# A hybrid attention and product-key layer on one core: three quarters of the modulation sums move from VectorE to column strips of TensorE

## The chip, the cores and the metric

The kernel runs on one core of one Trainium2 chip. The metric is the device time in microseconds (us) of one execution, as the median of several runs. Times inside the kernel come from one profiled execution; they are counted from its first instruction.

## What is computed

One decoder layer, float32, 256 tokens (T), width 2048 (D), weights read once from HBM. Cut to what matters here:

```python
c_act = jax.nn.silu(c)                              # one vector of 2048
mod = jnp.dot(c_act, w_ada) + b_ada                 # w_ada is 2048 x 12288, 96 MB
sh1, sc1, g1, sh2, sc2, g2 = split(mod, 6)          # 2048 each
h = layer_norm(x) * (1 + sc1) + sh1
mix = token_mix(h, ...)                             # w_in (32 MB), attention, w_o (16 MB)
x = layer_norm(alpha * x + g1 * mix, ln1_g, ln1_b)
h = layer_norm(x) * (1 + sc2) + sh2
ffn = peer(h, w_pq, ..., u_table, v_table)          # 16 MB, then two tables of 128 MB
out = layer_norm(alpha * x + g2 * ffn, ln2_g, ln2_b)
```

`token_mix` projects with `w_in` to the queries, keys and values of eight dilated heads ("a"), to the two latents of eight further heads ("b") and to a 64-wide rotary key (`kr`). `peer` scores every token against 128 x 128 keys, takes the top 16 of each head and mixes rows of `u_table` and `v_table`.

## The kernel before

**Products.** Two ways of multiplying float32 matrices stand side by side. In the split way, ScalarE (ACT) rounds a weight tile to `hi` (L98), VectorE (DVE) makes `lo = raw - hi` (L100), and TensorE (PE) makes three products (`mm3`, L137 to L139; for `u` two, L132 and L133). In the plain way PE multiplies the raw float32 tile (L330 for `w_in`, L147 and L154 for the latents), and ACT and DVE do nothing. A piece is 1 MB, 4 x 128 rows by 512 columns. `F32_PIECES = (4, 3, 2, 3)` says how many of the eight pieces of each of the four row groups (`kg`) of `w_in` go the plain way; `LAT_F32` names three latent products that do.

**Modulation.** `w_ada` comes as 96 tiles of 1 MB, one for each 128 of the 12288 outputs, with output on the partitions (`ada`, L203 to L209). DVE multiplies such a tile with `cb`, the silu of `c` spread over all partitions, and sums along the row: two SCALAR_TENSOR_TENSOR of 128x1024, whose sums go to `modc` and `modh`; `ada_bias` (L211 to L215) adds the halves and the bias. The tiles are spread over the program: 8 (shift and scale 1 of row group 0) before the first piece of `w_in`, 24 between its pieces for the groups 1 to 3, 48 (gate 1, shift and scale 2: `ada_rest`) pulled one at a time by `ada_pull` between pieces and heads, and the last of them in the `w_pq` stage, and 16 (gate 2) late, in the second half of the `u` stage. `modulate` (L294 to L307) makes `h` from the normalised x with them, and multiplies `h` with the 64 columns of `w_kr` into two PSUM banks.

**Order.** The stages are: x and `c` in; four row groups of `w_in` (`kg` 0 to 3); latents and attention; `w_o`; a layer norm; `w_pq`; then `u` and `v`, twice. The order of instructions on each engine is set by the framework's scheduler from the order of the text, the dependences and its own costs. All loads stand on one queue (SP), in order; a load waits until its buffer is free, and the loads behind it wait too. The `ada` tiles of `ada_rest` have two buffers. PSUM has eight banks: four `mm`, two `tr`, two `sm`.

The lines that the change and the prediction touch: `F32_PIECES`, `LAT_F32` (L41 and L50), `bank` (L70), `ada` (L203), `ada_rest` (L240), `modulate` (L294), `ada_in` and the calls behind it (L344 to L380), `latents` (L515), `scatter` (L892).

## Time and profile before

| | |
|---|---|
| time, median of 3 runs | 2075.01 us (2072.48 to 2075.48) |
| the profiled execution's own time | 2072.09 us |
| its span, first to last instruction | 2070.3 us |
| PE busy | 2002.6 us (97%) |
| DVE busy | 1434.0 us (69%) |
| ACT busy | 1027.9 us (50%) |
| HBM read | 473.4 MB, 239 GB/s over the span |
| mean granted clock of TensorE | 0.983 |

Busy shares are means over the whole span; the stages differ. Matmuls are pipelined, so that the records of neighbours overlap: the spacing of a run of matmuls is the price of one, and its mean duration is more than that. A float32 matmul of the plain way leaves two records (two passes, each with a weight load); one on split operands leaves one.

### The profile page before, as it was taken

To read this page: it belongs to the slowest core of one execution; us is meant where nothing else is said; L and a number is where in the kernel's file an instruction comes from. 1 tells how busy PE (TensorE), PEld (TensorE's weight loads), DVE (VectorE), ACT (ScalarE), POOL (GpSimd) and SP (SyncE) were. 2 spreads that over 40 slices of the span, in tenths; PEclk is the share of its full clock that TensorE was granted. 3 is DMA by queue.
4 is the path that set the end of the run, shared out by engine and by line. 5 is a ranking of instruction groups with operands and counts; after the bars stand their busy time and mean duration, and the time that the engine had idled before them with its cause. 6 is when DMAs were issued, how large, how long until landed. Compare 5 with 4: busy or idle time off the path is not lost.

```text
span 2070.3 us, 26806 instructions
## 1 busy us (share of the span) xinstructions
PE 2002.6 (97%) x10328; PEld 1672.8 (81%) x10329; DVE 1434.0 (69%) x2509; ACT 1027.9 (50%) x1478; POOL 0.2 (0%) x4
## 2 busy tenths in 40 slices
PE   6999998979999999999999999999999999999997
PEld 3567686769988888899888888888888888888886
DVE  7589978889799677677765454477766555445457
ACT  2323457445554877866444444454444454444441
POOL 0000000000000000000000000000000000000000
PEclk8999999989999999999999999999999999999999
DMA  9787887858445555666885555578876656555552
GB/s 364 314 328 311 328 323 262 345 234 318 184 157 190 194 212 193 224 204 214 291 280 190 198 188 198 188 266 306 300 286 244 224 205 235 192 202 184 203 203 102
DMA packets 100864, 496.13 MB, mean 240 GB/s; under 512 B 7792, under 2 KB 41728, under 8 KB 42880
## 3 DMA queue, kind: packets, MB, share of 16 engines
q1 hardware_dynamic: 100736, 494.41, 64.8%
q8 instruction: 81, 1.33, 0.2%
q14 instruction: 47, 0.39, 0.1%
HBM read 473.40 MB, written 20.98 MB: 239 GB/s over the span
## 4 chain that ended last, share of the span: by engine, by line
PE 93%; DVE 5%; ACT 1%; issue 0%; DMA 0%; SPq 0%; DVEq 0%; ACTq 0%
PE u_ps L132 23%; PE u_ps L133 12%; PE v_ps L138 11%; PE v_ps L137 11%; PE v_ps L139 11%; PE win_ps L330 3%; PE g_ps L914 3%; PE win_ps L138 2%; PE win_ps L139 2%; PE wpq_ps L138 2%; PE wpq_ps L139 2%; DVE ada L208 2%; PE wpq_ps L137 1%; PE win_ps L137 1%; PE wo_ps L139 1%; PE wo_ps L138 1%
## 5 line engine op out<-in xcount | busy, mean ns | idle before, releaser
L132 PE MATMUL u_ps<-act,hi_u 128*128 128x512 f32 x2048 | 727.8, 400 | 3.0 <-DVE W L779 3.0
L133 PE MATMUL u_ps<-act,lo_u 128*128 128x256 f32 x2048 | 574.0, 280 | 0.0
L100 DVE TENSOR_TENSOR lo_v<-raw_v,hi_v 128x1024 fp32r<-128x1024 f32 x244 | 298.2, 1224 | 264.4 <-ACT hi_v L98 264.3
L132 PEld LDWEIGHTS u_ps<-act,hi_u 128*128 128x128 f32 x2048 | 386.1, 189 | 95.2 <-DVE W L779 3.3
L100 DVE TENSOR_TENSOR lo_u<-raw_u,hi_u 128x1024 fp32r<-128x1024 f32 x256 | 312.1, 1222 | 179.8 <-ACT hi_u L98 178.8
L98 ACT CAST hi_v<-raw_v 128x1024 fp32r<-128x1024 f32 x244 | 257.2, 1054 | 327.8 <-PE v_ps L139 321.3
L133 PEld LDWEIGHTS u_ps<-act,lo_u 128*128 128x128 f32 x2048 | 387.6, 189 | 0.0
L137 PE MATMUL v_ps<-hi_v,whi 128*128 128x512 f32 x976 | 379.7, 389 | 0.0
L138 PE MATMUL v_ps<-lo_v,whi 128*128 128x512 f32 x976 | 379.7, 389 | 0.0
L139 PE MATMUL v_ps<-hi_v,wlo 128*128 128x512 f32 x976 | 379.7, 389 | 0.0
L98 ACT CAST hi_u<-raw_u 128x1024 fp32r<-128x1024 f32 x256 | 267.6, 1048 | 212.5 <-PE u_ps L132 193.4
L208 DVE SCALAR_TENSOR_TENSOR ada<-ada,cb 128x1024 f32<-128x1024 f32 x192 | 229.0, 1219 | 12.2 <-DMA ada<-in_w_ada_dram 12.0
L137 PEld LDWEIGHTS v_ps<-hi_v,whi 128*128 128x128 f32 x976 | 183.2, 188 | 38.3
L139 PEld LDWEIGHTS v_ps<-hi_v,wlo 128*128 128x128 f32 x976 | 183.2, 188 | 38.0
L138 PEld LDWEIGHTS v_ps<-lo_v,whi 128*128 128x128 f32 x976 | 183.2, 188 | 37.8
L330 PE MATMUL win_ps<-raw_win,hmod 128*128 128x512 f32 x192 | 87.2, 610 | 1.2 <-ACT hmod L301 1.2
L912 DVE TENSOR_SCALAR o<-iota,i2T,gT 128x128 f32<-128x128 f32 x256 | 72.9, 342 | 19.9 <-PE g_ps L914 19.8
L137 PE MATMUL wpq_ps<-act,hi_wpq 128*128 128x256 f32 x256 | 72.7, 286 | 1.9 <-ACT act L157 1.9
L138 PE MATMUL wpq_ps<-act,hi_wpq 128*128 128x256 f32 x256 | 73.1, 286 | 0.4 <-DVE act L158 0.4
L778 ACT COPY W<-u_ps 128x256 f32<-128x256 f32 x128 | 47.3, 369 | 52.3 <-PE u_ps L133 51.8
L139 PE MATMUL wpq_ps<-act,lo_wpq 128*128 128x256 f32 x256 | 72.8, 285 | 0.0
L330 PEld LDWEIGHTS win_ps<-raw_win,hmod 128*128 128x128 f32 x192 | 36.9, 196 | 43.8 <-issue 42.0
(319 smaller groups left out, 2316.1 us busy)
## 6 DMA issues: line engine op xcount, KB each, us to landing
raw_u<-in_u_dram SPq DMA_DIRECT2D x128, 1024.0 KB, 4.8
raw_v<-in_v_dram SPq DMA_DIRECT2D x122, 1024.0 KB, 4.8
ada<-in_w_ada_dram SPq DMA_DIRECT2D x96, 1024.0 KB, 5.9
raw_win<-in_w_in_dram SPq DMA_DIRECT2D x32, 1024.0 KB, 8.4
raw_wo<-in_w_o_dram SPq DMA_DIRECT2D x16, 1024.0 KB, 6.9
raw_wpq<-in_w_pq_dram SPq DMA_DIRECT2D x16, 1024.0 KB, 6.0
g_d<-stg SPq DMA_DIRECT2D x16, 1024.0 KB, 4.9
gl<-g_d SPq DMA_DIRECT2D x16, 1024.0 KB, 6.8
```

Of the source, the lines that this page charges most:

```text
L98: nc.scalar.copy(hi, raw[:, 2 * j:2 * j + 2, :])
L100: nc.vector.tensor_sub(lo, raw[:, 2 * j:2 * j + 2, :], hi.bitcast(F32))
L132: nc.tensor.matmul(pss[e], hi[:, i, es], act[:, k], start=first and j == 0 and i == 0, stop=False)
L133: nc.tensor.matmul(pss[e][:, 1], lo[:, i, es], act_hi[:, k, :], start=False, stop=last and j == 1 and i == 3)
L137: nc.tensor.matmul(o, sh, mh, start=start, stop=False)
L138: nc.tensor.matmul(o, sh, ml, start=False, stop=False)
L139: nc.tensor.matmul(o, sl, mh, start=False, stop=stop)
L208: nc.vector.scalar_tensor_tensor(w[:, z, :], w[:, z, :], 1.0, cb[:, z * 1024:(z + 1) * 1024], op0=ALU.mult, op1=ALU.mult, accum_out=(modc, ...
L330: nc.tensor.matmul(ps[th], act[:, i, ts], src[:, i, :], start=i == 0, stop=i == 3)
L778: nc.scalar.copy(ws[:, e], pss[e][:, 1])
L912: nc.vector.tensor_scalar(o2, iota, i2T[:, t:t + 1], gT[:, t:t + 1], op0=ALU.is_equal, op1=ALU.mult)
L914: nc.tensor.matmul(ps[:, q * P:(q + 1) * P], o1[:, q, :], o2, start=True, stop=True)
```

## The change

It touches four things.

1. `ada_group`: the 48 tiles of gate 1, shift 2 and scale 2 are laid out anew (`w_ada_r`: 128 rows x 4 row blocks x 512 columns, 1 MB a tile, 4 tiles for a group of 512 outputs). PE multiplies each row block of a tile (moving, 512 columns) with one column of `c1`, the silu of `c` (stationary, 1 column), into one row of a PSUM bank: row block g goes to partition 32 g, that is, to column strip g of the array. After 16 such matmuls ACT copies the bank to SBUF (`rows`), four small matmuls with `strips` (ones on the four partitions) add the strips and turn the row into columns, and DVE adds the bias.
2. `first_ada` does the same, in two halves, for the 8 tiles that come before the first piece of `w_in` (`w_ada0`, 256 columns, two strips for shift and two for scale). The 24 tiles of the row groups 1 to 3 and the 16 of gate 2 stay on DVE (`ON_PE = False`).
3. Seven pieces of `w_in` and the three latent products leave the plain way for the split one: `F32_PIECES` becomes (3, 1, 1, 0), `LAT_F32` becomes empty.
4. The bank `sm` is halved to one buffer and the other becomes `ad`, for the strips. So `kr` is now made transposed, in two strips of 64 columns in one bank (16 matmuls of 256 columns for 32 of 64), and turned back by two small matmuls; the heads' outputs (`o_`) have one bank for two; `scatter` uses `sm`, `tr`, `ad`, `tr` in turn.

```diff
-F32_PIECES = (4, 3, 2, 3)
+F32_PIECES = (3, 1, 1, 0)
+ON_PE = False
...
-LAT_F32 = ('uk0', 'uq1', 'uqr')
+LAT_F32 = ()
...
-        return psum.tile([P, 512], F32, tag=tag, name=name, bufs=4 if tag == "mm" else 2)
+        return psum.tile([P, 512], F32, tag=tag, name=name, bufs={"mm": 4, "tr": 2, "sm": 1, "ad": 1}[tag])
...
+    c1 = cols[:, V_C:V_C + KC]
...
+    def ada_group(ps, ws, tiles, strips, j0):
+
+        for q in range(4):
+            p, tag, bufs = tiles[q]
+            w = p.tile([P, 4, 512], F32, tag=tag, name=f"ada{j0}_{q}", bufs=bufs)
+            nc.sync.dma_start(w, ws[q])
+            for g in range(4):
+                nc.tensor.matmul(ps[32 * g:32 * g + 1, :], c1[:, 4 * q + g:4 * q + g + 1], w[:, g, :], start=q == 0,
+                                 stop=q == 3)
+            if q < 3:
+                yield
+        rows = stream.tile([P, 2, 512], F32, tag="lo", name=f"ada_rows{j0}", bufs=4)[:, 0, :]
+        nc.scalar.copy(rows, ps)
+        yield
+        for i in range(4):
+            nc.tensor.matmul(ps[:, 2 * i:2 * i + 2], rows[:, i * P:(i + 1) * P], strips[:, 2:4], start=True, stop=True)
+        one = 1.0 if (SC1 <= j0 < G1 or SC2 <= j0 < G2) else 0.0
+        nc.vector.scalar_tensor_tensor(modc[:, j0:j0 + 4], ps[:, 0:8:2], one, cols[:, j0:j0 + 4], op0=ALU.add,
+                                       op1=ALU.add)
+
+    def ada_rows(ps, w, which, half):
+
+
+        for i in range(8):
+            g = 32 * (2 * which + i % 2)
+            k = 8 * half + i
+            nc.tensor.matmul(ps[g:g + 1, :256], c1[:, k:k + 1], w[:, i, :], start=half == 0 and i < 2,
+                             stop=half == 1 and i >= 6)
...
         def ada_rest():
-            for j in range(G1, SH2):
-                ada(front, "ada", 2, j)
-                yield
...
+            order = [G1 + 4 * g for g in range(4)] + [j + 4 * g for g in range(4) for j in (SH2, SC2)]
+            for j0 in order:
+                yield from ada_group(ada_ps, a["w_ada_r"][j0 // 4], [(front, "ada", 2)] * 4, strips, j0)
...
                 for i in range(2 * half, 2 * half + 2):
-                    for th in range(2):
-                        nc.tensor.matmul(kr_ps[th][:, :64], h[:, i, th * P:(th + 1) * P], kw[:, i, :],
-                                         start=(kg == 0 and i == 0), stop=(kg == 3 and i == 3))
...
+                    g = 64 * (i % 2)
+                    nc.tensor.matmul(kr_ps[g:g + 64, :T], kw[:, i, :], h[:, i, :], start=(kg == 0 and i < 2),
+                                     stop=(kg == 3 and i >= 2))
...
-            for m in range(4):
-                ada_in(0, m)
+            first_ada(0)
             for n in range(2):
                 first[0, n] = load_piece(a["w_in"][0, n], f"win0_{n}")
-            for m in range(4, 8):
-                ada_in(0, m)
+            first_ada(1)
...
-                        ps = bank(("sm", "tr")[b % 2], f"g_ps{tb}_{b}")
+                        ps = bank(("sm", "tr", "ad", "tr")[b], f"g_ps{tb}_{b}")
```

What the diff does not show is where the new matmuls come to stand. The first place is PE in row group 3, between piece 7 and piece 0 of `w_in` (`win_ps3_n_th` is the bank of piece n and token half th). Before:

```order
L139 MATMUL win_ps3_7_1_1184<-hi_win3_7_1_1201,act_73 128x512
L137 MATMUL win_ps3_7_1_1184<-hi_win3_7_1_1201,act_73 128x512
L138 MATMUL win_ps3_7_1_1184<-lo_win3_7_1_1203,act_73 128x512
L139 MATMUL win_ps3_7_1_1184<-hi_win3_7_1_1201,act_73 128x512
L330 MATMUL win_ps3_0_0_1269<-raw_win3_0_1271,hmod3_1147 128x512 x2
L330 MATMUL win_ps3_0_1_1270<-raw_win3_0_1271,hmod3_1147 128x512 x2
```

And with the change:

```order
L139 MATMUL win_ps3_7_1_1327<-lo_win3_7_1_1346,act_73 128x512
L140 MATMUL win_ps3_7_1_1327<-hi_win3_7_1_1344,act_73 128x512
L233 MATMUL ada_ps_92<-ada32_0_1400,cols_67 1x512 x4
L233 MATMUL ada_ps_92<-ada32_1_1406,cols_67 1x512 x4
L596 MATMUL kr_ps_244<-both_1415,krT_1413 128x64 x2
L138 MATMUL win_ps3_0_0_1422<-hi_win3_0_0_1426,act_73 128x512
L138 MATMUL win_ps3_0_1_1423<-hi_win3_0_0_1426,act_73 128x512
L139 MATMUL win_ps3_0_0_1422<-lo_win3_0_0_1428,act_73 128x512
```

Two tiles of gate 1, four strip matmuls each, now stand in PE's row ahead of piece 0, which is now made from split operands.

The second place is PE in the `w_pq` stage, where the last tiles of `ada_rest` stand (`wpq_ps0` to `wpq_ps7` are the eight banks). Before there are only products of `w_pq`:

```order
L139 MATMUL wpq_ps1_3361<-act_73,lo_wpq0_1_0_3662 128x256
L137 MATMUL wpq_ps0_3360<-act_73,hi_wpq0_1_1_3664 128x256
L138 MATMUL wpq_ps0_3360<-act_73,hi_wpq0_1_1_3664 128x256
L139 MATMUL wpq_ps0_3360<-act_73,lo_wpq0_1_1_3666 128x256
L137 MATMUL wpq_ps0_3360<-act_73,hi_wpq0_1_1_3664 128x256
```

With the change:

```order
L233 MATMUL ada_ps_92<-ada76_1_4193,cols_67 1x512 x4
L233 MATMUL ada_ps_92<-ada76_2_4199,cols_67 1x512 x4
L138 MATMUL wpq_ps2_3813<-act_73,hi_wpq1_1_0_4227 128x256
L139 MATMUL wpq_ps2_3813<-act_73,hi_wpq1_1_0_4227 128x256
L138 MATMUL wpq_ps3_3814<-act_73,hi_wpq1_1_0_4227 128x256
L139 MATMUL wpq_ps3_3814<-act_73,hi_wpq1_1_0_4227 128x256
L233 MATMUL ada_ps_92<-ada76_3_4205,cols_67 1x512 x4
L241 MATMUL ada_ps_92<-strips_94,ada_rows76_4211 128x2 x4
L140 MATMUL wpq_ps2_3813<-act_73,lo_wpq1_1_0_4229 128x256
```

The load of tile `ada76_3` waits for the buffer that the matmuls on `ada76_1` give back, and only the four on `ada76_2` and four matmuls of 256 columns stand between; the four adding matmuls (L241) stand right behind the last strip matmul.

The third place is DVE in the same stage (`lo_wpqn_kg_j` is half j of a piece). Before:

```order
L100 TENSOR_TENSOR lo_wpq2_1_1_3812<-raw_wpq2_1_3804,hi_wpq2_1_1_3810 128x1024
L208 SCALAR_TENSOR_TENSOR ada78_3716,modc_71<-ada78_3716,cb_68 128x1024
L208 SCALAR_TENSOR_TENSOR ada78_3716,modh_72<-ada78_3716,cb_68 128x1024
L208 SCALAR_TENSOR_TENSOR ada63_3720,modc_71<-ada63_3720,cb_68 128x1024
L208 SCALAR_TENSOR_TENSOR ada63_3720,modh_72<-ada63_3720,cb_68 128x1024
L214 TENSOR_TENSOR modc_71<-modc_71,modh_72 128x4
L215 SCALAR_TENSOR_TENSOR modc_71<-modc_71,cols_67 128x4
```

With the change the two large instructions of a tile are gone; a group of four tiles leaves one small one:

```order
L101 TENSOR_TENSOR lo_wpq0_1_1_4143<-raw_wpq0_1_4135,hi_wpq0_1_1_4141 128x1024
L101 TENSOR_TENSOR lo_wpq1_1_0_4229<-raw_wpq1_1_4225,hi_wpq1_1_0_4227 128x1024
L243 SCALAR_TENSOR_TENSOR modc_71<-ada_ps_92,cols_67 128x4
L101 TENSOR_TENSOR lo_wpq1_1_1_4233<-raw_wpq1_1_4225,hi_wpq1_1_1_4231 128x1024
L101 TENSOR_TENSOR lo_wpq2_1_0_4294<-raw_wpq2_1_4290,hi_wpq2_1_0_4292 128x1024
```

The small instruction waits for PE's adding matmuls; the split of `w_pq` goes on around it.

## Rows read from the trace of the kernel before

**Rows 1.** The page's head: the span, and the busiest engine.

```profile
span 2070.3 us, 26806 instructions
PE 2002.6 (97%) x10328; PEld 1672.8 (81%) x10329; DVE 1434.0 (69%) x2509; ACT 1027.9 (50%) x1478; POOL 0.2 (0%) x4
```

**Rows 2.** Busy time by stage, 0 to 588 us; the first row names the columns.

```profile
core 0: us, PE busy (x) PEld busy (x) DVE busy (x) ACT busy (x) POOL busy (x), PEclk, DMA share, GB/s
0.00:28.00 28.00, 11.91 (x64) 9.98 (x64) 22.05 (x61) 10.41 (x18) 0.20 (x4) 0.82 0.85 340
28.00:90.00 62.00, 56.71 (x175) 34.02 (x176) 41.47 (x71) 20.95 (x33) 0.00 (x0) 0.92 0.85 340
90.00:142.00 52.00, 50.31 (x186) 33.34 (x185) 41.29 (x67) 13.52 (x17) 0.00 (x0) 1.00 0.86 351
142.00:196.00 54.00, 50.98 (x198) 36.26 (x197) 44.43 (x72) 17.14 (x20) 0.00 (x0) 0.97 0.84 342
196.00:251.00 55.00, 54.27 (x217) 37.16 (x217) 52.20 (x104) 23.55 (x42) 0.00 (x0) 1.00 0.71 271
251.00:342.00 91.00, 84.16 (x464) 65.55 (x462) 73.13 (x219) 55.45 (x133) 0.00 (x0) 0.98 0.81 313
342.00:450.00 108.00, 102.28 (x470) 83.17 (x469) 93.13 (x167) 53.36 (x77) 0.00 (x0) 0.97 0.77 302
450.00:475.00 25.00, 12.07 (x48) 8.30 (x48) 23.66 (x55) 15.69 (x26) 0.00 (x0) 0.65 0.46 177
475.00:588.00 113.00, 112.83 (x900) 110.98 (x900) 97.71 (x296) 56.17 (x70) 0.00 (x0) 0.99 0.62 234
```

**Rows 3.** Who waited, PE alone, 0 to 800 us: total, times, longest.

```profile
PE h_ps L712 <- ACT xc L709: 10.7, 2, 6.9
PE xnT_ps L291 <- issue: 9.4, 1, 9.4
PE win_ps L138 <- DVE lo_win L100: 5.6, 4, 2.9
...
PE pt_a L434 <- DVE mx_a L429: 4.9, 4, 3.6
```

**Rows 4.** The chain that ended last, runs of one kind: start, length, what.

```profile
90.39 1.73 PE kr_ps L306 x16
...
132.87 2.29 DVE ada L208 x4
...
258.00 1.73 PE uqr_ps L147 x4
...
270.86 1.73 PE uk_ps L154 x8
```

**Rows 5.** Busy time, `w_o` alone (400 to 425) and `w_pq` alone (500 to 525).

```profile
400.00:425.00 25.00, 25.00 (x112) 20.70 (x111) 22.69 (x30) 11.60 (x12) 0.00 (x0) 1.00 0.82 330
500.00:525.00 25.00, 25.00 (x208) 24.83 (x208) 19.15 (x29) 11.02 (x14) 0.00 (x0) 1.00 0.74 296
```

**Rows 6.** Timeline of PE, one score product: start, length, what.

```profile
285.32 0.70 PE L564 MATMUL s_b<-krT,qk 64*128 64x256 f32 x2
285.94 0.49 PE L561 MATMUL s_b<-qk 128*128 128x128 f32 x2
286.36 0.48 PE L562 MATMUL s_b<-krT,qk 64*128 64x128 f32 x2
286.78 0.70 PE L563 MATMUL s_b<-qk 128*128 128x256 f32 x2
```

**Rows 7.** Instructions on the tile `ada`, 0 to 600 us.

```profile
L208 DVE SCALAR_TENSOR_TENSOR ada<-ada,cb x160: 1161/1220/1226, 13.6 to 516.7; 128x1024 f32<-128x1024 f32 x160
...
DMA to landing us min/median/max: 4.7/6.7/15.2
```

**Rows 8.** Timeline of the start.

```profile
18.97 1.35 DVE L187 TENSOR_SCALAR xn<-xn,ln_mv,rs_r 128x2048 f32<-128x2048 f32 x1
...
27.51 1.09 ACT L301 ACTIVATE hmod<-xnT,modc 128x256 f32<-128x256 f32 x2
```

More of the change, by code (lines that the diff above doesn't have):

```diff
@@ L209, in ada, with silu_strips @@
                                            op1=ALU.mult, accum_out=(modc, modh)[z][:, j:j + 1])
+    c1 = cols[:, V_C:V_C + KC]
+    def silu_strips(pool):
+        ps = bank("ad", "ada_ps")
+        nc.vector.memset(ps, 0.0)
+        strips = pool.tile([P, 4], F32, name="strips")
+        nc.vector.memset(strips, 0.0)
+        for g in range(4):
+            nc.vector.memset(strips[32 * g:32 * g + 1, g // 2:g // 2 + 1], 1.0)
+            nc.vector.memset(strips[32 * g:32 * g + 1, 2:4], 1.0)
+        return ps, strips
+    def ada_group(ps, ws, tiles, strips, j0):
[3 more added lines that the diff above has]
+            nc.sync.dma_start(w, ws[q])
+            for g in range(4):
+                nc.tensor.matmul(ps[32 * g:32 * g + 1, :], c1[:, 4 * q + g:4 * q + g + 1], w[:, g, :], start=q == 0,
[16 more added lines that the diff above has]
+                             stop=half == 1 and i >= 6)
     def ada_bias(j0, n):
@@ L282, in tile_hybrid_peer_block @@
             nc.scalar.activation(cols[:, V_C:V_C + KC], cols[:, V_C:V_C + KC], AF.Silu)
+            ada_ps, strips = silu_strips(front)
             spread_cols(cb, cols[:, V_C:V_C + KC], "c")
@@ L297, in modulate @@
                 for j0 in (SH1, SC1):
-                    ada_bias(j0 + 4 * kg + 2 * half, 2)
+                    if kg > 0 and not ON_PE:
+                        ada_bias(j0 + 4 * kg + 2 * half, 2)
                 for i in range(2 * half, 2 * half + 2):
@@ L353, in ada_in, with first_ada @@
                 return ada((early_a, early_b)[m % 2], "raw", 1, j)
+            def first_ada(half):
+                ps = ada_ps
+                for part in range(2):
+                    ws = []
+                    for which in range(2):
+                        m = 4 * half + 2 * part + which
+                        where = (0, 2, 1, 0)[m // 2]
+                        pool, tag, bufs = ((front, "ada", 2), (mix, f"xt{m % 2}", 1),
+                                           ((early_a, early_b)[m % 2], "raw", 1))[where]
+                        w = pool.tile([P, 8, 256], F32, tag=tag, name=f"ada0_{m}", bufs=bufs)
+                        nc.sync.dma_start(w, a["w_ada0"][half, which, part])
+                        ws.append(w)
+                    for which in range(2):
+                        ada_rows(ps, ws[which], which, part)
+                rows = stream.tile([P, 2, 512], F32, tag="lo", name=f"first_rows{half}", bufs=4)[:, 0, :]
+                nc.scalar.copy(rows[:, :256], ps[:, :256])
+                for i in range(2):
+                    nc.tensor.matmul(ps[:, 256 + 2 * i:258 + 2 * i], rows[:, i * P:(i + 1) * P], strips[:, 0:2], start=True,
+                                     stop=True)
+                for which, (j0, one) in enumerate(((SH1, 0.0), (SC1, 1.0))):
+                    j = j0 + 2 * half
+                    nc.vector.scalar_tensor_tensor(modc[:, j:j + 2], ps[:, 256 + which:260:2], one, cols[:, j:j + 2],
+                                                   op0=ALU.add, op1=ALU.add)
             def group_start(kg):
@@ L375, in tile_hybrid_peer_block @@
                 m = 0
+                if ON_PE:
+                    slots = [(front, "ada", 2)] * 2 + [(mix, f"xt{m}", 1) for m in range(2)]
+                    work = [ada_group(ada_ps, a["w_ada_r"][j0 // 4 + kg + 1], slots, strips, j0 + 4 * kg + 4)
+                            for j0 in (SH1, SC1)]
+                    work = itertools.chain(*work)
                 for ns in IN_ORDER[kg]:
@@ L378, in tile_hybrid_peer_block @@
                     while m < ns[-1] + 1:
-                        ada_in(kg + 1, m)
+                        if ON_PE:
+                            next(work, None)
+                        else:
+                            ada_in(kg + 1, m)
                         m += 1
+                if ON_PE:
+                    for _ in work:
+                        pass
             early_pools.close()
@@ L529, in latents @@
                     nc.tensor.transpose(ps[:, th * P:(th + 1) * P], krd[:, th].rearrange("p j e -> p (j e)"), ident)
[L530 removed]
+                krT = krs
                 nc.scalar.copy(krT, ps[:, :T])
```

24 lines of the change are left out of this document (12 added, 12 removed).

## The prediction

> **What bounds the kernel now.** The page's head comes first: PE is busy for 2002.6 of 2070.3 us [rows 1], so only 68 us of the whole span are without PE work, and the reader should ask where these lie. The busy time by stage answers: the nine stages to 588 us add up to 535.5 us of PE, so 52.5 us of the 68 lie in this fifth of the span, 16 in the start and 13 in the layer norm at 450 [rows 2]. DVE is busy 489 us in the same stretch, but in no stage more than PE except the start and the layer norm. The list of waits then says what PE waited for. The two largest are chains of small steps (10.7 us for the normalised rows, 9.4 at the start); the waits for DVE's `lo` and for its share of the softmax come to 5.6 and 4.9 us [rows 3]. So DVE is nearly full and still holds PE up for only some 10 us; PE sets the pace, at a granted clock of 1.00 or nearly (2.4 GHz) in most stages; only the start and the layer norm, where PE had gaps, show 0.82 and 0.65, a mix of 1.2 and 2.4 GHz [rows 2]. What the change does to the time is therefore read from what it adds to PE and takes from it. From 588 us on nothing is added to PE; the turn of the banks in `scatter` gives each of its products a bank that was as long unused as before, so I cost that at nothing.
>
> **Prices.** In runs without waits the chain gives the plain way: 4 records of `uqr` in 1.73 us, 8 of `uk` in 1.73 [rows 4]. A matmul of 512 columns leaves two records, so it costs 0.86 us, one of 256 columns 0.43. Split operands: 112 matmuls in 25 us, 0.223 each for 512 columns, and 208 in 25 us, 0.120 for 256 [rows 5]. A matmul of 64 columns, plain, is 2 x 0.108 [rows 4]; there the weight load is the limit, so I use 0.22 for the small adding matmuls. An `ada` tile costs DVE 2.29 us [rows 4].
>
> **The change part by part.**
>
> Ten pieces off the plain way. A piece is 8 matmuls of 512 columns: 8 x 0.86 = 6.9 us plain, 24 x 0.223 = 5.4 split, 1.5 less. Seven pieces of `w_in` and `uqr` save 8 x 1.5 = 12.0. For `uk0` and `uq1`, 16 matmuls of 256 columns: 6.9 against 48 x 0.120 = 5.8, so 2.2 for both. **-14.2 us** of PE. DVE gets 20 `lo` for it, ACT 20 `hi`. In row groups 1 and 2 DVE goes from 41 and 44 us of 52 and 54 [rows 2] to about 46 and 47, still under PE; ACT has half of every stage free. Nothing for these.
>
> The key `kr`: 64 records at 0.108 = 6.9 us before; now 16 matmuls of 256 columns, 6.9 us one after the other or 3.5 if the two strips run together. **-3** (0 to -3.5).
>
> 48 tiles on strips: 192 matmuls of 512 columns with one stationary column. No row shows two strips at work, so the bounds are far apart: 192 x 0.86 = 165 us if they run one after the other, a quarter, **+41**, if four run together. I take 41: they use other columns of the array and other partitions of the bank, and the loads of weights already run beside matmuls (110.98 us busy beside 112.83 in `w_pq`, [rows 2]). What stands between the two is a rival below. The Trainium skill, "TensorE: Matmul & The Clock Gate" (Part 3), gives 2.38x for three column strips; at the same share of the ideal four would cost 52 us, 11 more, as an estimate; no run so far shows it.
>
> The adding matmuls: 48 at 0.22, **+10.5**.
>
> Changes of the array's shape. The score products switch between 64 rows and 128. The product of 256 columns over 64 rows starts at 285.32 and its successor at 285.94, 0.62 us for what costs 0.43 in the run of `uk`; the next ones take 0.42, where 0.22 would do [rows 4, 6]. So a switch costs 0.2 us. This is the rule that speaks against the change: the Trainium skill, "TensorEngine Tiling (Array Packing)" (Key Properties), says that changing the tiling mode drains the engine. The rows agree for strips of rows; by the rule this term would be 21 and the sum +52, without a drain nothing and the sum +31. The order of the changed kernel has 52 separate runs of strip matmuls among full ones, two switches each: 104 x 0.2 = 21 us. The stationary side is one column here and 128 there, which may make it cheaper. **+10** (0 to 21).
>
> Waits of PE for the tiles. DVE could fall behind a late tile; PE now stands still, and all its products behind. The load of a tile starts when the matmuls two tiles before are done, and lands after 6.7 us (4.7 to 15.2) [rows 7]. Counted in the order with the prices above, PE has over 6 us of work between the two in most cases, but 1 to 4 us in four, three of them in `w_pq` (one place is shown with the order): 2 to 5 us each. In three places the adding matmuls stand right behind the last strip, and wait for ACT's copy, some 1 us. **+10** (0 to 25).
>
> What DVE gives up: 56 tiles x 2.29 = 128 us. Of the 10.5 us that PE waited for DVE I take back most: **-8** (0 to -10.5). ACT's 14 extra copies and the single bank for the heads' outputs are hidden by the half of ACT that is free; without that cover the heads would wait some 0.5 us each, 8 us.
>
> The start. The normalising of x stood behind four tiles on DVE until 18.97, and the first `hmod` came at 27.51 [rows 8]. With the tiles on PE, which is idle there for 16 us [rows 2], only the loads remain: 2 MB of x and 4 MB of tiles at 340 GB/s are there by about 20. **-5** (0 to -8). The 64 small strip matmuls (64 x 0.43 / 4 = 7 us or more) lie in PE's idle time here; without that cover they are 7 us more.
>
> Sum: -14.2 -3 +41 +10.5 +10 +10 -8 -5 = **+41.3 us**. The profiled execution took 2072.1 us itself (span 2070.3), 2.9 under the median of 2075.0; with the change it would be 2113.4, and the median 2116.3. I say 2116. With all open terms at their low ends the sum is 41 + 10.5 - 14.2 - 3.5 - 10.5 - 8 = +15 (2090), at the high ends 41 + 10.5 - 14.2 + 21 + 25 = +83 (2158).
>
> **Rivals.**
>
> *The passes overlap only by halves.* Every plain matmul of the program is two records, x2 for one [rows 6], and the second pass of a strip needs the first out of the way. If PE starts them strictly in order, strip 1 starts with strip 0's second pass: a block of four takes five passes, 5 x 0.43 = 2.15 us for 0.86. 48 blocks cost 103 instead of 41: +62 on the sum, 2178. For it: the two records stand in program order; against it: nothing in the trace, it has no strips.
>
> *The strips do nothing.* The matmuls run one after the other, and the change does not do what it says: 165 for 41, 2240. Against it speaks that the shape is switched at all, since a switch is seen in the rows.
>
> *Faster: PE's waits close.* If DVE's load, not the chain of small steps, is what lies behind PE's gaps, the strips fill idle time instead of making the row longer. PE's net gain of work is +41 +10.5 -14.2 -3 = 34 us; there are 52.5 us of gaps to 588 [rows 2]. The point that decides is whether more than 34 of them close; if 47 do, the time is 13 less, 2062. For it: DVE at 80 to 95% in row groups and `w_o`, where a late `lo` stops PE. Against: 29 us of the gaps are the start and the layer norm, and the listed waits for DVE are 10.5 [rows 3].
>
> **How the numbers follow.** The measurement can tell about 0.2%, 4 us, from no change. Forecast 0.50, half overlap 0.21, no overlap 0.09, waits close 0.14, and 0.06 that terms cancel within 4 us: faster 0.14, same 0.06, slower 0.80. The range goes from 2060, which holds most of the faster case, over the forecast's own 2090 to 2158, to 2190, past the middle of half overlap; no overlap, and the far side of the two others, are left out, about 0.2.
>
> **What would show it.** In the profile after, the strip matmuls of one tile should start almost together and a block should take about 0.9 us, with a gap of some 0.2 on either side; 2.2 would be the first rival, 3.4 the second. PE's busy time to the `u` stage should grow by 35 to 60 us, most of it from row group 3 on, and that stage should begin near 630 instead of 588. DVE's should fall by some 100. In the list of waits, `ada_ps` waiting for its DMA should come to about 10 us, and PE's waits for `lo_win` be gone. If the `u` stage begins before 588, PE was not what bounded the front, and the reading of the stages was wrong.

## The result, and the profile after

The changed kernel takes 2148.3 us (median of 4 runs, 2145.8 to 2150.5) where the kernel before takes 2073.7 beside it on the same chip: a ratio of 1.036, with an interval of 1.0342 to 1.0378. The change costs 74.6 us. The forecast was 41.3, with the right sign and 2148 inside the range. What moved is 56 of the 96 tiles, 7 in 12, not the three quarters that the title names.

The page of the changed kernel, its head and the busy time of the engines, against [rows 1]:

```profile
span 2147.2 us, 28038 instructions
...
PE 2083.4 (97%) x11012; PEld 1701.9 (79%) x11013; DVE 1334.2 (62%) x2306; ACT 1055.9 (49%) x1513; POOL 0.2 (0%) x4
```

PE is busy for 80.8 us more than before, and DVE for 99.8 less. The span without PE work is 64 us; it was 68. So the change gave PE's row more work and closed hardly any of its gaps. The busy time by stage of the changed kernel, cut where the same instructions stand, shows in which stages this happened, against [rows 2]:

```profile
core 0: us, PE busy (x) PEld busy (x) DVE busy (x) ACT busy (x) POOL busy (x), PEclk, DMA share, GB/s
0.00:28.00 28.00, 19.75 (x132) 13.37 (x132) 14.29 (x53) 10.65 (x19) 0.20 (x4) 1.00 0.93 378
28.00:91.00 63.00, 59.45 (x243) 34.26 (x244) 33.95 (x53) 22.93 (x35) 0.00 (x0) 0.97 0.78 310
91.00:145.00 54.00, 49.30 (x197) 34.81 (x197) 46.54 (x73) 18.98 (x24) 0.00 (x0) 1.00 0.88 359
145.00:198.00 53.00, 49.04 (x196) 36.00 (x196) 46.71 (x74) 17.57 (x20) 0.00 (x0) 0.97 0.83 340
198.00:256.00 58.00, 56.54 (x284) 39.41 (x281) 37.87 (x69) 30.80 (x50) 0.00 (x0) 1.00 0.67 259
256.00:379.00 123.00, 118.27 (x738) 80.43 (x737) 48.48 (x178) 69.22 (x154) 0.00 (x0) 0.97 0.62 232
379.00:494.00 115.00, 112.99 (x562) 82.48 (x562) 65.63 (x106) 51.02 (x70) 0.00 (x0) 1.00 0.71 281
494.00:512.00 18.00, 9.81 (x51) 4.53 (x52) 16.78 (x45) 8.72 (x16) 0.00 (x0) 0.81 0.73 274
512.00:648.00 136.00, 125.27 (x921) 109.48 (x920) 65.92 (x191) 56.55 (x73) 0.00 (x0) 0.90 0.49 178
```

The start and the first three row groups are as long as before to 2 us: `kr` of group 3 begins at 197.6 (before 195.7). Then group 3 grows by 7 us, the attention by 23, `w_o` by 12. The layer norm stays. `w_pq` takes 136.5 us instead of 104.9, so it carries 32 of the 74. The `u` stage begins at 647.7 instead of 573.7, and from there to the end the two kernels differ by 3 us (1499.5 and 1496.6); in the kernels of this document, none of which differs there but by the banks of `scatter`, this part takes 1493 to 1501 us, so 3 us is no effect that can be told. The loss lies where the 48 tiles of `ada_rest` are pulled, as it should; but in `w_pq` it is largest, and there the granted clock is 0.90 where the same stage had 0.97 before. Over the whole stretch to the `u` stage the clock is not lower. Here it is in one row, first of the kernel before and then of the changed one:

```profile
0.00:573.70 573.70, 521.23 (x2626) 406.14 (x2628) 474.92 (x1038) 258.47 (x420) 0.20 (x4) 0.95 0.76 300
0.00:647.70 647.70, 600.13 (x3310) 434.50 (x3312) 375.87 (x835) 286.24 (x455) 0.20 (x4) 0.96 0.68 266
```

The kernel before has its half clock (1.2 GHz) mostly in the first 48 us and the layer norm, the changed one from the layer norm on. PE is busy at half clock for 36 us before and 42 after, so the clock costs 3 us more in all.

What PE waited for, 0 to 700 us, the largest entries of the changed kernel (total, times, longest), against [rows 3]:

```profile
PE win_ps L139 <- DVE lo_win L101: 9.8, 9, 3.4
PE h_ps L790 <- ACT xc L787: 8.7, 3, 6.3
PE ada_ps L233 <- DMA ada<-in_w_ada_r_dram: 6.3, 2, 3.2
...
PE ada_ps L241 <- ACT ada_rows L238: 3.9, 5, 1.6
```

The waits for `lo_win` were 5.6 us. They have grown, though DVE has 100 us less to do. New are the two entries on `ada_ps`: the strips wait for a tile, and the adding matmuls for ACT's copy. The instructions on that tile give the whole bill (name, records, their duration as minimum, median and maximum in ns, first and last start):

```profile
L233 PE MATMUL ada_ps<-ada,cols x384: 590/591/1061, 210.3 to 570.6; 128*1 128x512 f32 x192
...
L241 PE MATMUL ada_ps<-strips,ada_rows x96: 165/251/373, 228.6 to 573.8; 128*128 128x2 f32 x96
```

Taken from each record's start to the next one's, the strips hold PE for 72.2 us and the adding matmuls for 14.3. In 11.3 of the 72.2 PE stands idle behind a strip record, 8.2 of these in the layer norm, where its next product waits for ACT's `xc`; so 60.9 are work of the strips. The sections below take these apart.

### The profile page after: what moved, and what is told of

Its sections match the earlier page's. It is cut to its first block, busy times and chain, and to the rows that moved or that the text cites. A ratio compares the mean times of both kernels' runs of the same rounds, so it can differ in the third digit from the quotient of the medians.

```text
span 2147.2 us, 28038 instructions
## 1 busy us (share of the span) xinstructions
PE 2083.4 (97%) x11012; PEld 1701.9 (79%) x11013; DVE 1334.2 (62%) x2306; ACT 1055.9 (49%) x1513; POOL 0.2 (0%) x4
## 4 chain that ended last, share of the span: by engine, by line
PE 90%; DVE 5%; DMA 3%; ACT 1%; issue 1%; SPq 0%; DVEq 0%; ACTq 0%
PE u_ps L133 22%; PE u_ps L134 11%; PE v_ps L139 10%; PE v_ps L138 10%; PE v_ps L140 10%; PE g_ps L992 3%; PE ada_ps L233 2%; PE win_ps L139 2%; DMA gl<-g_d 2%; PE win_ps L140 2%; PE win_ps L138 2%; PE win_ps L368 2%; PE wpq_ps L140 2%; PE wpq_ps L138 1%; PE wpq_ps L139 1%; PE wo_ps L140 1%
## 5 line engine op out<-in xcount | busy, mean ns | idle before, releaser
L138 PEld LDWEIGHTS v_ps<-hi_v,whi 128*128 128x128 f32 x976 | 183.2, 188 | 37.9
L139 PE MATMUL win_ps<-lo_win,act 128*128 128x512 f32 x216 | 87.4, 405 | 10.2 <-DVE lo_win L101 9.8
L209 DVE SCALAR_TENSOR_TENSOR ada<-ada,cb 128x1024 f32<-128x1024 f32 x80 | 95.1, 1220 | 3.3 <-DMA ada<-in_w_ada_dram 3.2
L138 PE MATMUL win_ps<-hi_win,act 128*128 128x512 f32 x216 | 84.6, 406 | 2.5 <-ACT hi_win L99 2.5
L140 PE MATMUL win_ps<-hi_win,act 128*128 128x512 f32 x216 | 85.1, 394 | 0.0
L99 ACT CAST hi_win<-raw_win 128x1024 fp32r<-128x1024 f32 x54 | 54.8, 1050 | 53.2 <-DMA raw_win<-in_w_in_dram 36.7
L138 PE MATMUL wpq_ps<-act,hi_wpq 128*128 128x256 f32 x256 | 75.0, 295 | 0.0
L101 DVE TENSOR_TENSOR lo_win<-raw_win,hi_win 128x1024 fp32r<-128x1024 f32 x54 | 64.6, 1220 | 15.1 <-ACT hi_win L99 15.0
```

The source lines that it names most:

```text
L99: nc.scalar.copy(hi, raw[:, 2 * j:2 * j + 2, :])
L101: nc.vector.tensor_sub(lo, raw[:, 2 * j:2 * j + 2, :], hi.bitcast(F32))
L138: nc.tensor.matmul(o, sh, mh, start=start, stop=False)
L139: nc.tensor.matmul(o, sh, ml, start=False, stop=False)
L140: nc.tensor.matmul(o, sl, mh, start=False, stop=stop)
L209: nc.vector.scalar_tensor_tensor(w[:, z, :], w[:, z, :], 1.0, cb[:, z * 1024:(z + 1) * 1024], op0=ALU.mult, op1=ALU.mult, accum_out=(modc, ...
```

## Do the strips run together?

The forecast rested on it (41 us), and two rivals denied it (103 or 165). In the timeline of PE, one block in row group 3 of the changed kernel reads (start, length, what):

```profile
226.57 0.39 PE L140 MATMUL win_ps<-hi_win,act 128*128 128x512 f32 x1
226.89 1.04 PE L233 MATMUL ada_ps<-ada,cols 128*1 128x512 f32 x8
227.86 0.73 PE L138 MATMUL win_ps<-hi_win,act 128*128 128x512 f32 x2
```

Eight records, two for each of four strips, take 0.97 us from the first's start to the next product's, with what the switch costs. The starts of the eight show how: the first passes of the four strips begin 6 to 7 ns apart, then 408 ns later the four second passes begin, as close together. So the second pass of a strip doesn't hold back the first pass of the next one.

Not every block stays whole. Nine of the 48 are broken by other matmuls: one strip runs alone, and the other three follow later, as here in the attention:

```profile
259.77 1.02 PE L233 MATMUL ada_ps<-ada,cols 128*1 128x512 f32 x2 [0.32 <-DVE modc L243]
...
262.22 1.03 PE L233 MATMUL ada_ps<-ada,cols 128*1 128x512 f32 x6
```

The lone strip holds PE for 0.95 us and the three for 0.96, as long as a whole block. So the 48 blocks take 57 times two passes, 114 x 0.43 = 49 us and not the 41 of the forecast.

**One strip.** To see what the block costs without that, all sixteen matmuls of a group go into strip 0. The other three strips are then not written and keep what lay there; the work on PE is the same in number and size.

```diff
-                nc.tensor.matmul(ps[32 * g:32 * g + 1, :], c1[...], w[:, g, :], start=q == 0, stop=q == 3)
+                nc.tensor.matmul(ps[0:1, :], c1[...], w[:, g, :], start=q == 0 and g == 0, stop=q == 3 and g == 3)
```

> All 16 matmuls of a group of gate 1, shift 2 and scale 2 go to one column strip instead of four; the numbers of matmuls, copies and loads stay. If the four strips really ran together and this stands on the path (theory), 192 matmuls x 0.86 us come one after the other instead of four at a time: +124 us, about 2270 us, and a block of four takes 3.4 us instead of 0.9. If the loads or the waits of the tiles set the pace and not PE's time on them (rival), less than +40, below 2190.

It took 2235.7 us (one run; 2072.0 before beside it). The same place in PE's timeline:

```profile
236.08 0.39 PE L140 MATMUL win_ps<-hi_win,act 128*128 128x512 f32 x1
236.40 3.59 PE L233 MATMUL ada_ps<-ada,cols 128*1 128x512 f32 x8
239.92 0.50 PE L138 MATMUL win_ps<-hi_win,act 128*128 128x512 f32 x1
```

3.52 us instead of 0.97, records 428 to 429 ns apart. PE's time on L233 goes from 72.2 to 176.3 us, and the kernel takes some 87 us more than with four strips. That lies between the two expectations: PE's gaps ahead of the `u` stage close from 47.6 to 31.0 us, so part of the added time fills what was idle. Both rivals on the strips fall; four column strips gave four times the rate, 8 x 0.429 = 3.43 us of passes in about 0.86. The Trainium skill, "TensorE: Matmul & The Clock Gate" (Part 3), gives 2.38x for three column strips; for four float32 strips of one column these rows show 4.0, so its figure would have put 11 us too many on the sum for whole blocks.

**Half the columns.** The strip matmuls run over 256 of the 512 columns, so half of the sums are left out; loads, copies, adding matmuls and switches stay.

```diff
-                nc.tensor.matmul(ps[32 * g:32 * g + 1, :], c1[...], w[:, g, :], ...)
+                nc.tensor.matmul(ps[32 * g:32 * g + 1, :256], c1[...], w[:, g, :256], ...)
```

> The changed kernel with the strip matmuls of the 48 tiles over the first 256 of 512 columns alone: half of these sums are left out, so that the modulation is not the reference's. Loads, copies, adding matmuls and the number of switches stay; a block costs 0.43 us for 0.86. If PE's time on the strips is on the path (theory 1): 48 x 0.43 = 21 us faster than the changed kernel, 2128. If late tiles set the pace (theory 2): PE waits for what it saves, less than 8 us, above 2140.

2126.4 us, ratio 1.0259 [1.0241, 1.0278], against 1.036 for the change: 21 us of 2073 come back. The strip records, per instruction of this kernel:

```profile
L233 PE MATMUL ada_ps<-ada,cols x384: 377/377/631, 212.2 to 554.5; 128*1 128x256 f32 x192
```

Each is 0.214 us shorter, and 114 passes give 24 us of PE time. By the medians 21 come back, in the two profiled executions 17 up to the `u` stage (630.4 for 647.7), and not where the passes lie. Forty of the 48 blocks lie ahead of `w_pq`, some 20 us of the saving; that stage begins at 505.5 instead of 511.2, so only 5.7 of it arrive there. In `w_pq` lie eight blocks, some 4 us; the stage takes 124.9 instead of 136.5, 11.6 less. So ahead of `w_pq` part of the strips' time is covered (three blocks, 4.7 us of work, lie in the gaps of the layer norm), and in `w_pq` they cost more than their own length, which the section on the waits takes up.

**No adding.** The 48 adding matmuls go, and DVE takes every second of the first eight columns of ACT's copy in place of their sums, so the sums over the strips are left out.

```diff
-        for i in range(4):
-            nc.tensor.matmul(ps[:, 2 * i:2 * i + 2], rows[:, i * P:(i + 1) * P], strips[:, 2:4], start=True, stop=True)
...
-        nc.vector.scalar_tensor_tensor(modc[:, j0:j0 + 4], ps[:, 0:8:2], one, ...)
+        nc.vector.scalar_tensor_tensor(modc[:, j0:j0 + 4], rows[:, 0:8:2], one, ...)
```

> The changed kernel without the 48 adding matmuls: VectorE takes its columns from ScalarE's copy of the strips, so that the modulation of gate 1, shift 2 and scale 2 is not the reference's. Loads, strip matmuls and copies stay. In the profile after, the adding matmuls take 14.3 us of PE, and PE waits some 6 us for the copy ahead of them, partly at half clock. If their PE time and these waits are on the path (theory 1): 15 to 22 us faster than the changed kernel, 2126 to 2133. If they fill time that PE waits through anyway (theory 2): less than 6 us, above 2142.

2131.2 us, ratio 1.0285 [1.0267, 1.0303]: 15 us back (0.0075 of 2073). Again the sum is near what the records hold PE in the trace of the change, 14.3, and the places are others: `w_pq` begins 3.4 us earlier, though nine of the twelve groups lie ahead of it, and itself takes 120.8 us instead of 136.5. The busy time of this kernel over `w_pq` and its neighbours, to set beside the row 512 to 648 above:

```profile
512.00:635.00 123.00, 116.72 (x921) 105.52 (x921) 70.78 (x223) 56.09 (x70) 0.00 (x0) 0.97 0.53 193
```

The granted clock is 0.97 here and 0.90 in the change. Without the adding matmuls the tiles run otherwise against PE's row: PE waits 4.0 us for tiles in `w_pq` instead of 6.3, with one long wait instead of two. So this run measures the adding matmuls together with the waits that they help to bring about.

## Which part costs what

Five kernels take parts off the change, one, two or three of them. Each time is given with its ratio to the kernel before, run beside it.

**First eight tiles back on DVE.**

```diff
-                    if kg > 0 and not ON_PE:
+                    if not ON_PE:
...
-            first_ada(0)
+            for m in range(4):
+                ada_in(0, m)
...
-            first_ada(1)
+            for m in range(4, 8):
+                ada_in(0, m)
```

> The changed kernel with the first 8 tiles on VectorE again; the 48 tiles stay on strips, the ten pieces split, kr in strips. In the profile after, the second half of row group 0 began 4 us later than before, because the strip matmuls of the second four tiles stand behind w_in pieces 0 and 1 on PE. If that is what the first tiles cost (theory 1): about 4 us faster than the changed kernel, 2144. If PE gives the time back later (theory 2): no difference, 2146 to 2150.

2145.0, 1.0343 [1.0326, 1.0361]. On PE the first tiles cost some 3.5 us, within the two intervals; that they gain is not shown.

**The ten pieces plain again.**

```diff
-F32_PIECES = (3, 1, 1, 0)
+F32_PIECES = (4, 3, 2, 3)
...
-LAT_F32 = ()
+LAT_F32 = ('uk0', 'uq1', 'uqr')
```

> The changed kernel with the ten pieces in the plain float32 way again, as before. By PE's arithmetic of the prediction (theory 1) they cost PE 14 us more: 2162 us. If the split pieces only swap PE time for waits on DVE's lo and ACT's hi in the row groups (theory 2), no difference beyond 4 us, or faster: 2140 to 2152, with row groups 1 and 2 as long as now (53 us each).

2154.1, 1.0398 [1.0377, 1.0418]: splitting the ten pieces gains 8 us (0.0038 of 2073), with intervals that just overlap. It lies between the two expectations.

**The 48 tiles back on DVE,** the ten pieces split as in the change.

```diff
-            order = [G1 + 4 * g for g in range(4)] + [j + 4 * g for g in range(4) for j in (SH2, SC2)]
-            for j0 in order:
-                yield from ada_group(ada_ps, a["w_ada_r"][j0 // 4], [(front, "ada", 2)] * 4, strips, j0)
+            for j in range(G1, SH2):
+                ada(front, "ada", 2, j)
+                yield
+            ada_bias(G1, 16)
...
```

> The changed kernel with the 48 tiles of gate 1, shift 2 and scale 2 on VectorE again; the first 8 tiles stay on strips and the ten pieces stay split. If PE's time on the strips is the whole loss (theory 1) the 77 us go and the split pieces bring their 14: 2060 us. If split pieces and 48 tiles together are too much for DVE (theory 2: 20 lo more, 24 us, on an engine that was 80 to 95% busy from row group 0 to w_o), it lies above the kernel before: 2080 to 2100.

2084.3, 1.0064 [1.0044, 1.0084], as by the second theory. Against it the 48 tiles on strips, with the pieces split (1.036), cost 0.0296 of 2073, 61 us.

**The 48 tiles back and the pieces plain,** so that the first eight tiles, the key and the banks are left of the change.

```diff
-F32_PIECES = (3, 1, 1, 0)
+F32_PIECES = (4, 3, 2, 3)
...
-                yield from ada_group(ada_ps, a["w_ada_r"][j0 // 4], [(front, "ada", 2)] * 4, strips, j0)
+                ada(front, "ada", 2, j)
...
```

> The kernel before with only the first 8 tiles and kr on strips: the 48 tiles on VectorE and the ten pieces plain, as before. The prediction's term for the start (theory 1) says 5 us faster and kr 3: 2066 us. If the loads and not VectorE set the start (theory 2, the profile after shows the first w_in matmul at 28.2 as before), no difference beyond 4 us: 2070 to 2078.

2079.7, 1.0042 [1.003, 1.0054], above both expectations, with single executions from 2075.7 to 2084.2. Against this the 48 tiles on strips, with the pieces plain (1.0398), cost 0.0356 of 2073, **74 us**. And the ten pieces, split while DVE has the tiles (1.0064), cost 4.6 us, in intervals that overlap, instead of gaining 8: a gain shows only once DVE has lost the tiles.

**The key and the banks alone:** the same, and the first eight tiles back on DVE too.

```diff
-            first_ada(0)
+            for m in range(4):
+                ada_in(0, m)
...
```

> The kernel before with the bank change alone: kr transposed in two strips, one bank for the heads' outputs, scatter's banks in turn; all tiles on VectorE, the ten pieces plain. The kernel with the first 8 tiles on strips as well was 8 us slower than before. If those 8 us are the first tiles' (theory 1): no difference from before, 2069 to 2075. If the bank change costs (theory 2: one bank for the heads' outputs, a longer chain for krT): 2076 to 2080.

2076.1, 1.0011 [1.0001, 1.002], +2.3 us; inside what can be told from no change. In its trace `kr` itself does what was forecast: the eight records of a row group take 1.0 us where sixteen took 1.73 [rows 4], 2.9 us less for four groups. But turning the key back takes 0.6 us, and PE's waits ahead of `kr` grow from 3.5 to 5.0 us, so 0.8 of the 2.9 are left. What takes these and the 2.3, the single banks or something else, the runs don't tell. From here to the kernel with the first tiles too it is 6 us (0.0031 of 2073).

Taken in this order, each step from the kernel of the one ahead of it, the steps are +2 for banks and key, +6 for the first tiles, +74 for the 48 tiles and -8 for the pieces, which by construction is the whole 74.6. In another order the prices are others (61 instead of 74 for the tiles with the pieces split).

## Why the pieces gave so little

Four of them lie in row groups 0 to 2, three in group 3, three in the latent projections. Three kernels split these.

**Groups 0 to 2 plain again in the change.**

```diff
-F32_PIECES = (3, 1, 1, 0)
+F32_PIECES = (4, 3, 2, 0)
```

> The changed kernel with the four pieces of row groups 0 to 2 in the plain way again (4, 3, 2, 0); the three of group 3 and the three latent products stay split. The kernel with all ten back was 6 us slower, and its row group 3 began at 196.9 us against 197.6, so that the four seem to give nothing. If split pieces of these groups only swap PE time for waits on lo (theory 1): within 3 us of the changed kernel, 2145 to 2151. If PE's arithmetic holds there too (theory 2): 4 x 1.45 = 6 us slower, 2154.

2145.6, 1.0356 [1.0338, 1.0375]: no difference to 1.036. Four pieces, 6 us of PE work by the forecast, are worth nothing. The waits of PE in groups 1 and 2 show where it went, first of the changed kernel (91 to 198 us), then of the kernel before (90 to 196):

```profile
PE win_ps L139 <- DVE lo_win L101: 7.2, 4, 3.4
PE win_ps L138 <- ACT hi_win L99: 1.2, 2, 0.7
```

```profile
PE win_ps L138 <- DVE lo_win L100: 4.5, 2, 2.9
```

Groups 1 and 2 take 53 to 54 us in both kernels. In the change PE is busy 49 of these and DVE 46.5; the split pieces need a `hi` and a `lo` each, and they come later than PE could use them. Three pieces less are 4.5 us of PE work, and the waits grew by 7.2 + 1.2 - 4.5 = 3.9: the saved work became waiting. Beside the kernel with all ten plain (1.0398 [1.0377, 1.0418]) this one shows what the other six pieces are worth without the tiles on DVE: 0.0042 of 2073, 9 us, with intervals that don't overlap.

**The latent pieces split in the kernel before.**

```diff
-LAT_F32 = ('uk0', 'uq1', 'uqr')
+LAT_F32 = ()
```

> The kernel before with the three latent products split and nothing else. PE's arithmetic (theory 1) gives 3.7 us (1.5 for uqr, 1.1 each for uk0 and uq1): 2069 us. If DVE, 80% busy there with the tiles, passes the 6 more lo on to PE as waits (theory 2): no difference or slower, 2072 to 2077.

2075.4, 1.0019 [1.0009, 1.0029], +4 us: no gain while DVE has the tiles.

**Group 3's pieces split in the kernel before.**

```diff
-F32_PIECES = (4, 3, 2, 3)
+F32_PIECES = (4, 3, 2, 0)
```

> The kernel before with the three plain pieces of row group 3 split and nothing else. PE's arithmetic (theory 1) gives 3 x 1.5 = 4.4 us: 2068 us. DVE is at 95% in that stage (52.2 of 55 us), and 6 more lo are 7.3 us of it; if that is passed on to PE (theory 2): 2073 to 2080.

2082.3, 1.005 [1.0034, 1.0066]: 10 us slower, more than either theory had, for 4.5 us of PE work saved. Row group 3 of this kernel, its busy time and then PE's waits (195 to 260 us):

```profile
196.00:251.00 55.00, 48.51 (x210) 38.30 (x210) 50.44 (x95) 27.48 (x46) 0.00 (x0) 0.94 0.63 239
```

```profile
PE krT_ps L529 <- DVE krd L526: 2.4, 1, 2.4
PE win_ps L138 <- DVE lo_win L100: 2.1, 4, 0.6
PE lt_kv_ps L477 <- ACT proj L236: 1.9, 2, 1.7
```

DVE is busy 92% of the stretch and PE 88%. From `kr` of group 3 to the end of `w_in` it takes 59.8 us instead of 51.8. PE's waits there, 0.7 us in the kernel before, are 6.4, of which 4.5 are for DVE; and the clock, 1.00 before, is at half in two stretches of 3.4 us. That DVE has become the limit of the stage is argued from these rows. This one edit costs more than all ten pieces do in the kernel with the new start (4.6), so the prices don't add up from one kernel to the next. In the changed kernel DVE is free there (37.9 of 58 us), and there the pieces of group 3 and the latent ones bring the 9 us.

## Waits for the tiles, and the clock behind them

`w_pq` grew by 31.6 us. The records of strips and adding take 18.9 of them and the waits ahead of these 9.6 (6.3 for tiles, 3.0 for ACT's copies, 0.3 for DVE); the projection's own products, which did not change, take 4.0 more than before. PE's timeline of the changed kernel around one late tile (in brackets, the idle time before and what ended it):

```profile
539.08 0.28 PE L139 MATMUL wpq_ps<-act,hi_wpq 128*128 128x256 f32 x1
542.43 1.88 PE L233 MATMUL ada_ps<-ada,cols 128*1 128x512 f32 x8 [3.07 <-DMA ada<-in_w_ada_r_dram]
545.02 1.86 PE L241 MATMUL ada_ps<-strips,ada_rows 128*128 128x2 f32 x8 [0.71 <-ACT ada_rows L238]
546.75 0.56 PE L140 MATMUL wpq_ps<-act,lo_wpq 128*128 128x256 f32 x1
547.11 0.41 PE L138 MATMUL wpq_ps<-act,hi_wpq 128*128 128x256 f32 x1
547.32 0.41 PE L139 MATMUL wpq_ps<-act,hi_wpq 128*128 128x256 f32 x1
```

PE stands for 3.1 us for the tile, one of the places that were counted from the order, and 0.7 for the copy. But the block then takes 1.9 us instead of 1.0, and products of 256 columns come 0.21 us apart, where [rows 5] gives 25 / 208 = 0.120. The granted clock is 0.5 of full (1.2 GHz) from 541.5 us, within the wait, to 551.7, and again from 568.8 to 579.0 around the end of the second such wait (3.2 us). The two stretches:

```profile
541.50:551.70 10.20, 8.56 (x37) 4.85 (x38) 3.56 (x4) 0.59 (x1) 0.00 (x0) 0.50 0.55 218
568.80:579.00 10.20, 8.55 (x38) 6.59 (x39) 1.55 (x3) 4.00 (x7) 0.00 (x0) 0.50 0.24 80
```

So two waits of 3.1 and 3.2 us each came with 10.2 us at half clock, in which PE was busy for 8.6: some 4.3 us lost, more than the wait itself. Not every wait of this length brings as much: behind the 3.4 us for `lo_win` that end at 168.7 the clock is at half for 3.4 us. The prediction priced the waits (three in `w_pq`, 2 to 5 us each) and not what follows them. The whole stage in the kernel before, to compare with the row 512 to 648 above:

```profile
469.00:574.00 105.00, 102.64 (x829) 100.67 (x828) 89.19 (x237) 52.78 (x67) 0.00 (x0) 0.97 0.67 255
```

105 x 0.97 = 102 us at full clock before, 136 x 0.90 = 122 after: of the 31 us, 20 are work and waits at the same clock and 11 are the clock. Most of the 11 lies in the strips' and adding matmuls' own records: by the prices at full clock (20 passes at 0.43, 24 adding records at 0.108, 0.1 for the switch behind each of eight runs of strips) their 18.9 us would be 12.

The new layout is not what makes the tiles late: a tile of `w_ada_r` lands 4.8 us after its issue (median of 48), one of the kernel before after 5.9.

**Pull the tiles earlier.** If the late tiles in `w_pq` are the trouble, the strips can be pulled in `w_o` instead, and none is left for `w_pq`.

```diff
-PULL_WO = (2, 3, 0, 1, 1, 1, 1, 1, 0, 0, 1, 2)
+PULL_WO = (2, 3, 1, 2, 2, 2, 2, 2, 2, 2, 2, 2)
```

> The changed kernel with more tiles pulled in the w_o stage, so that no strip matmul stands in the w_pq stage (13 tiles did). That stage was 31.6 us longer than before: 13 x 1.26 us of PE for tiles (0.86 block, 0.19 switches, 0.21 adding) are 16.4, the rest waits for late tiles and for ACT's copy and PE at half clock behind them. If only the tiles' own time moves and the waits go (theory 1): 10 to 18 us faster than the changed kernel, 2130 to 2138. If the waits only move along with the tiles (theory 2): within 4 us, 2144 to 2152.

2156.6, 1.0406 [1.0388, 1.0423], 9 us slower than the change and above both expectations. (By the trace of the change eight tiles stood in `w_pq` and three in the layer norm, not thirteen in `w_pq`.) The stages `w_o`, layer norm and `w_pq` of this kernel:

```profile
381.00:534.00 153.00, 138.00 (x674) 89.89 (x672) 65.56 (x108) 52.10 (x72) 0.00 (x0) 0.93 0.72 272
534.00:553.00 19.00, 6.87 (x29) 5.50 (x30) 18.32 (x49) 10.29 (x18) 0.00 (x0) 0.60 0.29 114
553.00:658.00 105.00, 102.73 (x832) 100.86 (x831) 64.78 (x188) 53.81 (x68) 0.00 (x0) 0.97 0.46 166
```

`w_pq` is back at its 105 us and its clock of 0.97, which shows that nothing but the tiles had lengthened it. But `w_o` takes 153 us instead of 115, and there the same thing happens, in PE's timeline of this kernel:

```profile
418.88 1.90 PE L233 MATMUL ada_ps<-ada,cols 128*1 128x512 f32 x16 [0.32 <-DVE modc L243]
...
425.41 1.88 PE L233 MATMUL ada_ps<-ada,cols 128*1 128x512 f32 x8 [4.63 <-DMA ada<-in_w_ada_r_dram]
427.90 1.89 PE L233 MATMUL ada_ps<-ada,cols 128*1 128x512 f32 x8 [0.61 <-DMA ada<-in_w_ada_r_dram]
```

With 22 tiles in `w_o` instead of 11, two buffers run dry: 4.6 us of waiting, and single blocks (x8) of 1.9 us at half clock. The three tiles that the change had in the layer norm, where PE has gaps anyway, have lost that cover too. Whether a third buffer would make the waits go wasn't tried.

## The start

The prediction gave the first eight tiles a gain of 5 us. The timeline of the changed kernel, against [rows 8]:

```profile
15.06 1.35 DVE L188 TENSOR_SCALAR xn<-xn,ln_mv,rs_r 128x2048 f32<-128x2048 f32 x1
...
22.25 1.09 PE L328 MATMUL xnT_ps<-ident,xn 128*128 128x128 f32 x8
23.28 2.76 PE L252 MATMUL ada_ps<-ada,cols 128*1 128x256 f32 x30
...
27.56 1.09 ACT L339 ACTIVATE hmod<-xnT,modc 128x256 f32<-128x256 f32 x2 [1.10 <-DVE modc L415]
...
36.97 4.51 PE L252 MATMUL ada_ps<-ada,cols 128*1 128x256 f32 x64
...
41.41 0.65 PE L344 MATMUL kr_ps<-hmod,kw 128*64 128x256 f32 x2
```

The normalising of `x` came 4 us earlier, at 15.06, as forecast. But `hmod` came at 27.56, where it had been at 27.51: it now waits for the modulation (`modc`) out of the strips, and the fourth tile lands at 18.9 us, against 19.2 before. The loads had been the limit beside DVE, and behind them the path through strips, copy and adding matmuls took what DVE had saved: the last strips, 30 records from 23.28 on, stand in PE's row behind the transposes of `x` (L328), 4.4 us after their tile has landed. Then the second four tiles: their 64 records stand in PE's row from 36.97 to 41.5, with no idle time to cover them, and the first product of `kr` comes at 41.4 instead of 37.3.

## Why the forecast came out short

The direction, the bound and the place were right: PE sets the pace, most of the added PE work goes into the time, DVE's 100 us give little back. The sum was 33 us short. By the prediction's own terms:

- **Ten pieces, -14.2:** measured -8, and +4.6 while DVE has the tiles. The step that failed is "still under PE ... Nothing for these": a mean of 46 busy us in 54 does not say that each `lo` is there when PE wants it. The waits for `lo_win`, forecast to be gone, went from 5.6 to 9.8 us.
- **The key, -3:** its records give 2.9, its waits and the turning back take 2.1 of them, and with the banks the part measures +2, within the noise. "A bank that was as long unused" is not shown wrong; where the 5 us between -3 and +2 lie stays open but for the 2.1.
- **48 tiles on strips, +41:** right for a whole block (0.86 us). But nine blocks are broken, 114 passes and not 96, which is 8 us more; the prediction counted these breaks for the changes of shape, in its 52 runs, and not for the passes. With the switch behind each run and the stretches at half clock the strips' records are 60.9 us of work. That it all lies on the path was too simple: 4.7 us of it lie in the layer norm's gaps, and halving the columns gave back, ahead of `w_pq`, 5.7 of 20.
- **Adding matmuls, +10.5:** right at full clock (96 x 0.108 = 10.4); 13.1 of work in the trace, since three of the twelve groups stood in stretches at half clock, at 0.213 us a record. The run without them gives 15, but with other waits.
- **Changes of shape, +10:** right. A product in front of strips holds PE for 0.32 us (226.57 to 226.89 above) where 0.223 is its price, and the last record of a block for 0.52 instead of 0.43; 0.19 for each of 52 runs, 10 us. The Trainium skill, "TensorEngine Tiling (Array Packing)" (Key Properties), has the drain and no number; for strips of one column it is half of what [rows 6] gave for the score products.
- **Waits for tiles, +10:** the waits themselves were well placed and sized (6.3 us for DMAs, 3.9 for the copy, forecast about 10). What failed is that a wait was priced at its own length: the clock costs `w_pq` 10 us more than before. Over the whole front it costs 3 us more, since the first 48 us have less of it than before.
- **DVE's waits taken back, -8:** no run measures it alone, but two traces that differ by the 48 tiles alone do: the kernel with the first eight tiles, key and banks alone has 46.4 us of PE gaps up to the `u` stage; with the 48 tiles on strips too (the ten pieces plain) it has 42.3, of which 10.3 are waits ahead of the tiles' own matmuls. So some 14 came back, 6 more than forecast, and of more kinds than the two that the prediction listed.
- **The start, -5:** +3.5 to +6. The step that failed is that the strips lie "in PE's idle time here"; that holds for the first four tiles and not for the second four, which the prediction mentioned as the price without cover and did not count.

The missing 33 us are thus: 6 from the pieces, 5 from banks and key, some 10 from the start, and 10 from the 48 tiles. These last are the broken blocks (8) and the clock (in the same two traces PE is busy at half clock for 25 and 39 us up to the `u` stage, 7 lost), less the 6 that came back beyond the forecast. The range held the result by luck as much as by design: of its room above, 34 us lay in the changes of shape, the waits and what DVE gives back, and 21 of the missing 33 us lie in the pieces, the key and the start, which had 8. The rival of closing waits did not meet its condition: it wanted more than 34 us of PE's gaps to close, and to the `u` stage they went from 52.5 to 47.6.

Two readings of the rows before were off. The stretch to 588 us is 28% of the span, not a fifth. And the `u` stage begins at 573.7 us and not at 588, so "near 630" should have read 615; it begins at 647.7. PE's busy time up to it grew by 78.9 us, where the prediction had 35 to 60.

No version here beats the kernel before. The nearest, the banks and the key alone, is equal to it.

## What to carry to other kernels

Work moved from an engine that has time left to the one that sets the pace is paid there, even at four times the rate: a tile took DVE 2.29 us beside other work and takes PE 61 / 48 to 74 / 48 us, 1.3 to 1.5, of the end-to-end time, with switches, adding, waits and clock. Count passes from the order in which the matmuls come to stand: strips that other work pulls apart are paid one by one. On an engine that works in order, price a wait for a transfer at its length plus what the engine does at the lower clock behind it. And a saving on one engine counts only where its feeder has time left at that very place: ask for the stage, with the waits, not for the sum of busy time.

## What was unexpected in the hardware

- Float32 matmuls of one stationary column in four column strips ran at 4.0 times the rate of one strip (0.86 us of passes for a block instead of 3.43). Each has two passes, and the second passes of all four ran together as well: first passes 6 to 7 ns apart, second passes 408 ns later.
- Between strips of one column and the full array a switch cost 0.1 us each way, half of what the switch between 64 and 128 rows cost in the score products [rows 6].
- A strip that other matmuls cut off from its block took 0.95 us alone, the other three 0.96, and all four together 0.97.
- Waits of 3.1 and 3.2 us for tiles, in a stage where PE was otherwise full, each came with 10.2 us at a granted clock of 0.5, before it was back at 1.00; a wait of 3.4 us for `lo_win` came with 3.4.
